# Operands of float32r products at multiples of 128 bytes; tables and masks of the second block made in the first block

## The chip, the cores and the metric

The kernel runs on one core of one Trainium2 chip. A time is the device time of one execution in microseconds (us); lower is better. Several executions are timed, and one is also recorded by the hardware profiler. TensorE (PE) multiplies matrices, with weight loads (PEld) beside it; VectorE (DVE), ScalarE (ACT) and GpSimd (POOL) do the element work; SyncE (SP) issues the DMAs. The on-chip buffer in which all operands of a product lie has 128 partitions; the offset of a tile is its start address within a partition.

## The reference

Two blocks are computed one after the other on 256 tokens of width 1024, two layers each. The first block has a context stream and a latent stream; its mixer joins attention, gated linear attention (GLA) and a convolution, and a gated feed-forward follows. The second block has a mixer of three kinds of attention and a feed-forward with a short convolution. It turns positions into rotary tables.

```python
def first_block(x, c, ctx, ...):
    ...
        x = _post(x, _latent_mixer(_modulate(x, sh1, sc1), mem, cos, sin, p), g1, ln1_g[l], ln1_b[l])
        x = _post(x, _ffn(_modulate(x, sh2, sc2), p), g2, ln2_g[l], ln2_b[l])
...
def second_block(x, positions, ...):
    cos, sin = rope_tables(positions)
    for l in range(DEPTH):
        h = rms_norm(x, attn_pre_norm[l])
        mix = hybrid_mixer(h, cos, sin, w_in[l], ...)
        x = x + rms_norm(mix, attn_post_norm[l])
        h = rms_norm(x, ffn_pre_norm[l])
        x = x + rms_norm(conv_ffn(h, w_up[l], ...), ffn_post_norm[l])
    return x
```

Here `_ffn` is `(silu(h @ w_gate) * (h @ w_up)) @ w_down` with a hidden width of 2816, and `rope_tables` is the cosine and sine of positions times eight frequencies.

## The kernel before

**Products in three parts.** A float32 product is made of three products in the type float32r. Each operand is split into a high part `hi` (rounded to float32r) and a low part `lo` (what is left), and `mm3` (L217) adds hi·hi (L220), hi·lo (L221) and lo·hi (L222) up in one PSUM tile. Weights come from DRAM in pieces of 128x1024 float32 (512 KB): `load` (L188) has SP start the DMA into one of four buffers `raw`; `weights` then has ScalarE cast it to `hi` (L210, three buffers) and VectorE subtract to `lo` (L213, two buffers, in halves of 512 columns). Activations are kept split too, as a pair of tiles in the buffer `b16`, which the profile calls `b`.

**Two shapes.** `gemm_f` takes 128 columns of weights as the stationary operand and streams 256 tokens of activations past it (out is channels by tokens; the profile's `g<-b,hi` with 128x256). `gemm_t` holds 128 tokens of activations and streams 512 columns of weights (`g<-hi,b` with 128x512). In names such as `g<-b,hi` out stands first, then the streamed operand, then the one that is held. Where activations of a feed-forward are in tiles `z`, `zz` or `h`, these stand in place of `b`; weights of the first block's feed-forwards also lie in free tiles `z`, `w` and `gp`.

**Pools and offsets.** Tiles lie in pools: `wts` (raw, hi, lo), `cst` and `sml` (constants and small tiles), `com` (b16 and rows), and one pool per stage: `first`, `mix0`/`mix1` (mixers), `ff`/`fx` (the feed-forwards of layers 0 and 1), `sec0` (second block). Within a pool tiles follow one another without gaps, so a tile of a width that isn't a multiple of 128 bytes moves those behind it. Where the built program puts the operands of the products, in bytes modulo 128 and modulo 256:

| operand | before, mod 128 | before, mod 256 | changed, mod 128 | changed, mod 256 |
|---|---|---|---|---|
| `hi`, `lo` in `wts` | 0 | 128 | 0 | 128 |
| `b` in `com` | 64 | 64 | 0 | 0 |
| `z` in `ff`, `w` and `zz` in `fx`, `hi` in `first` | 96 | 224 | 0 | 0 or 128 |
| tiles of the mixers in `mix` | 96 | 96 or 224 | 0 | 0 or 128 |
| `h` and others in `sec0` | 32 | 160 | 0 | 0 or 128 |
| `U` and others at the front of `first` | 64 | 192 | 0 | 0 or 128 |

**Order.** A scheduler with a timeline of its own decides the order of instructions on each engine when the program is built; code order and priorities guide it. Each engine then runs its row strictly in order, and SP issues DMAs in its row's order.

**The end of a mixer** (`post`, L1006 to L1051): for each of two token tiles and two halves of 512 columns, VectorE multiplies the product with the gate (L1019) and adds it to the residual (L1020); ScalarE squares it for the variance (L1024); GpSimd and VectorE make mean and inverse deviation of single columns (L1023 to L1034), and VectorE normalises (L1049, L1051). `ln` (L968, L976) normalises again for the next stage, and TensorE transposes (L991).

**Constants of the second block.** `positions` (L320) loads the positions, makes angles in eleven small VectorE operations and takes sine and cosine on ScalarE (L346, L347), which needs a table load. `consts2` (L349) casts the identity to bf16 (`identb`) and loads and casts two masks (`cmb`). Both are called at the start of the second block.

Of the kernel before, what the change touches and what calls it, by code (L numbers as in the profile page):

```python
# [9 lines left out]
F32 = mybir.dt.float32  # L10
F32R = mybir.dt.float32r
BF16 = mybir.dt.bfloat16
I32 = mybir.dt.int32
# [12 lines left out]
def together(**groups):  # L26
# [23 lines left out]
    'pt': dict(t=4),  # L50
}


# [112 lines left out]
class Core:  # L166
# [4 lines left out]
    def tile(self, pool, shape, dt=F32, tag=None, bufs=None):  # L171

        self.n += 1
        kind = pool.name.rstrip('0123456789')
        tag = SHARE.get(kind, {}).get(tag, tag)
        n = bufs or BUFS[kind].get(tag, 1)
        return pool.tile(list(shape), dt, name=f"{tag}_{self.n}", tag=tag, bufs=n)

# [138 lines left out]
class Second(Core):  # L317


    def positions(self, pos):  # L320
        nc = self.nc
        pi = self.tile(self.S, [128, 2], I32, 'pi')
        with nc.allow_non_contiguous_dma(reason="256 positions"):
# [4 lines left out]
        for t in range(2):  # L328
            nc.vector.tensor_scalar(ang[:, t], self.c('freq'), pf[:, t:t + 1], None, op0=ALU.mult)
        k = self.tile(self.S, [128, 2, 8], F32, 'angk')  # L330
# [18 lines left out]
    def consts2(self, cm):  # L349

        nc = self.nc
        self.identb = self.tile(self.P, [128, 128], BF16, 'identb')
        nc.vector.tensor_copy(self.identb, self.ident)
        self.cmb = []
        raw = self.load(cm)
        for t in range(2):
            b = self.tile(self.P, [128, 512], BF16, f'cmb{t}')
            nc.vector.tensor_copy(b, raw[:, t * 512:t * 512 + 512])
            self.cmb.append(b)
# [135 lines left out]
    def rope(self, pr, h0, n):  # L495
        nc = self.nc
        for t in range(2):
            x = pr[t][:, h0 * 64:(h0 + n) * 64].rearrange("p (h d) -> p h d", d=64)
            x1, x2 = x[:, :, 0:8], x[:, :, 8:16]
            cos = self.cs2[:, 0, t][:, None, :].to_broadcast([128, n, 8])  # L500
            sin = self.cs2[:, 1, t][:, None, :].to_broadcast([128, n, 8])
            a, b, c, d = [self.tile(self.P, [128, 14, 8], F32, 'rp')[:, :n] for _ in range(4)]
            nc.vector.tensor_mul(a, x1, cos)
            nc.vector.tensor_mul(b, x2, sin)
            nc.vector.tensor_mul(c, x2, cos)
            nc.vector.tensor_mul(d, x1, sin)
            nc.vector.tensor_sub(x1, a, b)
            nc.vector.tensor_add(x2, c, d)
# [203 lines left out]
    def attend(self, proj, pr, v, rb, src):  # L712
# [3 lines left out]

        ga = self.tile(self.P, [128, 2, 8, 3], F32, 'ga')
        lf, e, z = [self.tile(self.P, [128, 2, 4], F32, 'lf') for _ in range(3)]
        for t in range(2):
# [967 lines left out]
def build(tc, I, out):  # L1687
    nc = tc.nc
# [3 lines left out]
    with ExitStack() as es:  # L1692
# [16 lines left out]
        for l in range(2):  # L1709
            L = Layer1(l, I[f'w1{l}'], LAYOUT[0][l], I[f'row1{l}'])  # L1710
            L.a2 = I[f'a2{l}']
            L.vec = K.tile(K.C, [128, I[f'vec1{l}'].shape[1]], F32, 'vec1')
            nc.sync.dma_start(L.vec, I[f'vec1{l}'])
            L.cb2 = K.tile(K.C, [128, 8], F32, 'cb2')
            nc.vector.tensor_scalar(L.cb2, L.v('cb', 8), 2.0, None, op0=ALU.mult)
            Ls.append(L)
        with ExitStack() as e1:
# [18 lines left out]
            for l, L in enumerate(Ls):  # L1736
# [14 lines left out]
                with ExitStack() as e2:  # L1751
                    K.P = pool(e2, 'fx' if l else 'ff')
                    if l == 0:
# [3 lines left out]
                        for f in half:  # L1757
                            f()
                    else:
                        K.pend = left(K.ffn(L, X))  # L1760
        K.more = None
        with ExitStack() as e1:
# [7 lines left out]
            K.c = lambda n: c2[:, AT2[n][0]:AT2[n][0] + AT2[n][1]]  # L1770
            K.consts2(I['cm'])
            K.positions(I['pos'])
            for l in range(2):
# [17 lines left out]
```

## Time and profile before

| | us |
|---|---|
| median of 3 executions | 2732.79 |
| their range | 2726.75 to 2738.06 |
| profiled execution | 2729.63 |
| span of its instructions | 2727.8 |

The mean granted clock of TensorE in the profiled execution was 0.981 of full speed. In the profile the time of an engine is the sum of its instructions; TensorE's matmuls are pipelined, so the recorded duration of one is longer than the distance from its start to the next start. The chain that ended last is followed back from the last instruction, at each step to what released it. A number in brackets behind an instruction of the timeline is the idle time of its engine before it, with what ended it.

### The profile page before, as it was taken

How to read it: one execution, taken by the hardware profiler on the slowest of the kernel's cores; microseconds unless marked ns; L12 is line 12 of the kernel's file. 1: busy time of each engine (PE TensorE's matmuls, PEld its weight loads, DVE VectorE, ACT ScalarE, POOL GpSimd, SP SyncE). 2: the span in 40 equal slices, each digit the busy share in tenths (PEclk: the TensorE clock that was granted, in tenths of full speed). 3: DMA queues.
4: the chain of work that ended last, by engine and by line, in shares of the span. 5: the costliest groups of instructions: out<-in, count | busy, mean ns of one | idle time of the engine just before them, and what ended most of it. 6: DMA issues, size and time to landing. Idle time of an engine off the chain costs nothing.

```text
span 2727.8 us, 45641 instructions
## 1 busy us (share of the span) xinstructions
PE 2621.6 (96%) x17408; PEld 2271.2 (83%) x17408; DVE 1954.7 (72%) x3942; ACT 1383.3 (51%) x2524; POOL 137.8 (5%) x280
## 2 busy tenths in 40 slices
PE   7999999999999999999999999989989999999999
PEld 5977999977989888887797898979976699776997
DVE  4988977899967633355688997666676689556895
ACT  3555555545555422234754654544454566544663
POOL 0010011000001100001100100010010000000000
PEclk8999999999999999999999999989999999999999
DMA  7566456565535422222455433545554355542454
GB/s 255 187 224 206 163 178 211 185 208 180 179 116 206 173 93 93 93 93 100 154 167 201 160 120 117 172 152 186 186 183 148 110 170 196 172 160 93 163 193 155
DMA packets 127915, 443.34 MB, mean 163 GB/s; under 512 B 14888, under 2 KB 19112, under 8 KB 127696
## 3 DMA queue, kind: packets, MB, share of 16 engines
q1 hardware_dynamic: 127696, 440.43, 47.8%
q8 instruction: 137, 2.24, 0.3%
q14 instruction: 82, 0.67, 0.1%
HBM read 435.09 MB, written 5.28 MB: 161 GB/s over the span
## 4 chain that ended last, share of the span: by engine, by line
PE 88%; DVE 3%; DMA 3%; ACT 3%; issue 1%; POOL 1%; SPq 0%; DVEq 0%; POOLq 0%; ACTq 0%
PE g L221 21%; PE g L220 21%; PE g L222 20%; PE t L220 3%; PE t L222 3%; PE t L221 3%; DMA raw<-in_w_dram 3%; PE g L925 2%; PE t L1175 1%; PE t L1149 1%; PE t L1277 1%; PE t L1262 1%; PE t L1112 1%; PE t L1184 1%; PE g L663 1%
## 5 line engine op out<-in xcount | busy, mean ns | idle before, releaser
L213 DVE TENSOR_TENSOR lo<-raw,hi 128x512 fp32r<-128x512 f32 (+2 forms) x1280 | 824.8, 684 | 358.0 <-issue 157.3
L210 ACT CAST hi<-raw 128x1024 fp32r<-128x1024 f32 (+2 forms) x644 | 672.4, 1046 | 731.3 <-PE g L221 256.6
L220 PE MATMUL g<-b,hi 128*128 128x256 f32 (+1 forms) x2912 | 833.5, 288 | 4.4 <-ACT hi L210 3.9
L221 PE MATMUL g<-b,hi 128*128 128x256 f32 (+1 forms) x2912 | 829.4, 286 | 2.6 <-DVE b L311 2.5
L222 PE MATMUL g<-b,lo 128*128 128x256 f32 (+1 forms) x2912 | 823.4, 288 | 1.1 <-DVE lo L213 1.1
L220 PEld LDWEIGHTS g<-b,hi 128*128 128x128 f32 x2912 | 548.9, 189 | 15.1 <-ACT hi L210 4.3
L221 PEld LDWEIGHTS g<-b,hi 128*128 128x128 f32 x2912 | 549.4, 189 | 12.0 <-DVE b L311 3.9
L222 PEld LDWEIGHTS g<-b,lo 128*128 128x128 f32 x2912 | 542.1, 188 | 10.3 <-DVE lo L213 1.9
L1289 DVE SCALAR_TENSOR_TENSOR yc<-yc,vec,yc 128x256 f32<-128x256 f32 x720 | 345.4, 480 | 10.8
L221 PE MATMUL g<-lo,b 128*128 128x512 f32 (+2 forms) x712 | 271.4, 382 | 2.0 <-DVE lo L213 2.0
L222 PE MATMUL g<-hi,b 128*128 128x512 f32 (+2 forms) x712 | 264.7, 372 | 0.5 <-DVE b L314 0.4
L220 PE MATMUL g<-hi,b 128*128 128x512 f32 (+2 forms) x712 | 254.1, 377 | 11.2 <-ACT hi L210 5.7
L220 PEld LDWEIGHTS g<-hi,b 128*128 128x128 f32 x712 | 133.8, 191 | 38.5 <-ACT hi L210 6.5
L221 PEld LDWEIGHTS g<-lo,b 128*128 128x128 f32 x712 | 135.7, 191 | 30.7 <-DVE lo L213 6.2
L222 PEld LDWEIGHTS g<-hi,b 128*128 128x128 f32 x712 | 135.5, 190 | 22.2 <-DVE b L314 1.1
L220 PE MATMUL t<-b,hi 128*128 128x256 f32 (+1 forms) x336 | 112.6, 335 | 0.0
L221 PE MATMUL t<-b,hi 128*128 128x256 f32 (+1 forms) x336 | 112.6, 335 | 0.0
L222 PE MATMUL t<-b,lo 128*128 128x256 f32 (+1 forms) x336 | 112.4, 335 | 0.0
L477 DVE SCALAR_TENSOR_TENSOR s<-g,vec,s 128x255 f32<-128x255 f32 (+1 forms) x176 | 84.0, 478 | 6.0 <-ACT s L475 3.9
L925 PE MATMUL g<-raw,cs 128*32 128x256 f32 x768 | 67.7, 432 | 19.0 <-DMA raw<-in_w_dram 18.8
L221 PEld LDWEIGHTS t<-b,hi 128*128 128x128 f32 x336 | 63.7, 190 | 7.3
L220 PEld LDWEIGHTS t<-b,hi 128*128 128x128 f32 x336 | 63.2, 188 | 7.4
(421 smaller groups left out, 3928.7 us busy)
## 6 DMA issues: line engine op xcount, KB each, us to landing
raw<-in_w_dram SPq DMA_DIRECT2D x772, 512.0 KB, 3.8
b<-in_row_dram SPq DMA_DIRECT2D x16, 512.0 KB
b<-in_ctx_dram SPq DMA_DIRECT2D x4, 512.0 KB
ends<-st SPq DMA_DIRECT2D x8, 256.0 KB
st<-ends SPq DMA_DIRECT2D x8, 256.0 KB
b<-in_x_dram SPq DMA_DIRECT2D x4, 512.0 KB, 5.5
b<-ctx SPq DMA_DIRECT2D x4, 512.0 KB
raw<-in_w_dram SPq DMA_DIRECT2D x4, 426.0 KB
```

What stands on the lines that cost most here:

```text
L210: self.nc.scalar.copy(hi[:, :m], p)
L213: self.nc.vector.tensor_sub(lo[:, q], p[:, q], hi[:, q].bitcast(F32))
L220: t.matmul(ps, a[0], b[0], start=first, stop=False)
L221: t.matmul(ps, a[0], b[1], start=False, stop=False)
L222: t.matmul(ps, a[1], b[0], start=False, stop=last)
L477: nc.vector.scalar_tensor_tensor(c[:, m, j:], ps[:, m, :256 - j], cw[:, ft, 2 - j:3 - j], c[:, m, j:], op0=ALU.mult, op1=ALU.add)
L663: nc.tensor.matmul(ps[:, b], qk['nq', a * per + b][s, t * 128:t * 128 + 128], qk[kn, 0][s, :nk], start=False, stop=b == per - 1)
L925: m = nc.tensor.matmul(ps[32 * q:32 * q + 32, n * 256:n * 256 + 256], self.cs[:, h * 4 + q], raw[:, q * 256:q * 256 + 256], start=h == 0, ...
L1112: nc.tensor.matmul(p[:, h], kw[:, d, h * 128:h * 128 + 128], vg[:, h * 256:h * 256 + 256], start=True, stop=True)
L1149: nc.tensor.matmul(o, w, self.U[d][:, b * 256:b * 256 + n], start=d + i == 0, stop=d + i == 2)
L1175: nc.tensor.matmul(ps[:, a, h], G[h][b][:, a] if b < 3 else kT[:, h, ts], G[h][b][:, 2 + a], start=True, stop=True)
L1289: e.scalar_tensor_tensor(o, y[:, j:j + 256], w[:, j:j + 1], o, op0=ALU.mult, op1=ALU.add)
```

## The change

Tiles with two dimensions in the pools `first`, `mix`, `ff`, `fx` and `sec` are made wider, up to the next multiple of 128 bytes, and used in their first columns; three tiles that had more dimensions are written as padded two-dimensional ones, and `cb2` in `cst` gets 16 columns in place of 8. A scratch area at the front of the buffer is made 4096 bytes per partition in place of 16384. `consts2` and `positions` are called ahead of the feed-forward of the first block's second layer, and their tiles go to the pool `cst`; the frequencies get a DMA of their own.

```diff
--- before.py
+++ after.py
@@ -49,6 +49,11 @@
     'pg': dict(g=4),
     'pt': dict(t=4),
 }
+
+
+
+ALIGN = 128
+ALIGNED = ('first', 'mix', 'ff', 'fx', 'sec')
 
 
 class Layout:
@@ -174,7 +179,12 @@
         kind = pool.name.rstrip('0123456789')
         tag = SHARE.get(kind, {}).get(tag, tag)
         n = bufs or BUFS[kind].get(tag, 1)
-        return pool.tile(list(shape), dt, name=f"{tag}_{self.n}", tag=tag, bufs=n)
+        make = lambda s: pool.tile(s, dt, name=f"{tag}_{self.n}", tag=tag, bufs=n)
+        size = {F32: 4, F32R: 4, I32: 4, BF16: 2, U8: 1}[dt]
+        if kind in ALIGNED and len(shape) == 2 and shape[1] * size % ALIGN:
+            step = ALIGN // size
+            return make([shape[0], -(-shape[1] // step) * step])[:, :shape[1]]
+        return make(list(shape))
 
     @contextmanager
     def later(self, n):
@@ -317,8 +327,10 @@
 class Second(Core):
 
 
-    def positions(self, pos):
-        nc = self.nc
+    def positions(self, pos, freq):
+        nc = self.nc
+        fq = self.tile(self.S, [128, 32], F32, 'freq')[:, :8]
+        nc.sync.dma_start(fq, freq)
         pi = self.tile(self.S, [128, 2], I32, 'pi')
         with nc.allow_non_contiguous_dma(reason="256 positions"):
             nc.sync.dma_start(pi, pos.rearrange("o (t p) -> p (o t)", p=128))
@@ -326,7 +338,7 @@
         nc.vector.tensor_copy(pf, pi)
         ang = self.tile(self.S, [128, 2, 8], F32, 'ang')
         for t in range(2):
-            nc.vector.tensor_scalar(ang[:, t], self.c('freq'), pf[:, t:t + 1], None, op0=ALU.mult)
+            nc.vector.tensor_scalar(ang[:, t], fq, pf[:, t:t + 1], None, op0=ALU.mult)
         k = self.tile(self.S, [128, 2, 8], F32, 'angk')
         big = 1.5 * 2.0 ** 23
         nc.vector.tensor_scalar(k, ang, 1.0 / (2 * math.pi), big, op0=ALU.mult, op1=ALU.add)
@@ -349,12 +361,12 @@
     def consts2(self, cm):
 
         nc = self.nc
-        self.identb = self.tile(self.P, [128, 128], BF16, 'identb')
+        self.identb = self.tile(self.C, [128, 128], BF16, 'identb')
         nc.vector.tensor_copy(self.identb, self.ident)
         self.cmb = []
         raw = self.load(cm)
         for t in range(2):
-            b = self.tile(self.P, [128, 512], BF16, f'cmb{t}')
+            b = self.tile(self.C, [128, 512], BF16, f'cmb{t}')
             nc.vector.tensor_copy(b, raw[:, t * 512:t * 512 + 512])
             self.cmb.append(b)
 
@@ -499,7 +511,7 @@
             x1, x2 = x[:, :, 0:8], x[:, :, 8:16]
             cos = self.cs2[:, 0, t][:, None, :].to_broadcast([128, n, 8])
             sin = self.cs2[:, 1, t][:, None, :].to_broadcast([128, n, 8])
-            a, b, c, d = [self.tile(self.P, [128, 14, 8], F32, 'rp')[:, :n] for _ in range(4)]
+            a, b, c, d = [self.tile(self.P, [128, 112], F32, 'rp').rearrange("p (h n) -> p h n", n=8)[:, :n] for _ in range(4)]
             nc.vector.tensor_mul(a, x1, cos)
             nc.vector.tensor_mul(b, x2, sin)
             nc.vector.tensor_mul(c, x2, cos)
@@ -714,8 +726,8 @@
         nc = self.nc
         proj(5)
 
-        ga = self.tile(self.P, [128, 2, 8, 3], F32, 'ga')
-        lf, e, z = [self.tile(self.P, [128, 2, 4], F32, 'lf') for _ in range(3)]
+        ga = self.tile(self.P, [128, 48], F32, 'ga').rearrange("p (t h n) -> p t h n", h=8, n=3)
+        lf, e, z = [self.tile(self.P, [128, 8], F32, 'lf').rearrange("p (t h) -> p t h", h=4) for _ in range(3)]
         for t in range(2):
             nc.vector.tensor_add(z[:, t], pr[t][:, P2['ff']:P2['ff'] + 4], rb[:, 0:4])
             nc.vector.tensor_add(ga[:, t].rearrange("p h j -> p (h j)"), pr[t][:, P2['ng']:P2['ng'] + 24], rb[:, 4:28])
@@ -1711,7 +1723,7 @@
             L.a2 = I[f'a2{l}']
             L.vec = K.tile(K.C, [128, I[f'vec1{l}'].shape[1]], F32, 'vec1')
             nc.sync.dma_start(L.vec, I[f'vec1{l}'])
-            L.cb2 = K.tile(K.C, [128, 8], F32, 'cb2')
+            L.cb2 = K.tile(K.C, [128, 16], F32, 'cb2')[:, :8]
             nc.vector.tensor_scalar(L.cb2, L.v('cb', 8), 2.0, None, op0=ALU.mult)
             Ls.append(L)
         with ExitStack() as e1:
@@ -1757,6 +1769,9 @@
                         for f in half:
                             f()
                     else:
+                        K.consts2(I['cm'])
+                        n, m = AT2['freq']
+                        K.positions(I['pos'], I['cst2'][:, n:n + m])
                         K.pend = left(K.ffn(L, X))
         K.more = None
         with ExitStack() as e1:
@@ -1768,8 +1783,6 @@
             c2 = K.tile(K.P, list(CST2.shape), F32, 'cst2')
             nc.sync.dma_start(c2, I['cst2'])
             K.c = lambda n: c2[:, AT2[n][0]:AT2[n][0] + AT2[n][1]]
-            K.consts2(I['cm'])
-            K.positions(I['pos'])
             for l in range(2):
                 K.layer(X, K.vec2[l], I[f'w2{l}'], LAYOUT[1][l], I[f'row2{l}'], rows(out) if l else None)
             for t in range(2):
@@ -1780,7 +1793,7 @@
     import concourse.bacc as bacc
     from concourse.bass_utils import run_bass_kernel_spmd
 
-    nc = bacc.Bacc("TRN2", target_bir_lowering=False, num_devices=1)
+    nc = bacc.Bacc("TRN2", target_bir_lowering=False, num_devices=1, dynamic_dma_scratch_size=4096)
     ins = {f"in_{k}_dram": v for k, v in arrays({k: np.asarray(v) for k, v in inputs.items()}).items()}
     I = {k[3:-5]: nc.dram_tensor(k, v.shape, mybir.dt.from_np(v.dtype), kind="ExternalInput").ap() for k, v in ins.items()}
     out = nc.dram_tensor("out_0_dram", (256, D), F32, kind="ExternalOutput").ap()
```

The built program has as many instructions on TensorE, VectorE, ScalarE and GpSimd as before; SP has one DMA more. TensorE's row is the same but for a few neighbouring products of GLA in the first block's second mixer. Lines of the changed kernel stand 10 to 13 lines lower in the file (L1019 of before is L1031).

VectorE at the end of the mixer that precedes the last feed-forward of the first block (some 1795 to 1801 us of the profile), before:

```order
L1019 TENSOR_TENSOR th_18823<-g_18745,b_3106_18741 128x512
L213 TENSOR_TENSOR lo_18851<-raw_18848,hi_18850 128x512 x2
L1019 TENSOR_TENSOR th_18831<-g_18746,b_3106_18741 128x512
L1020 SCALAR_TENSOR_TENSOR b_1720_10318,pmv_18743<-b_1720_10318,th_18823 128x512
L213 TENSOR_TENSOR lo_19025<-raw_19022,hi_19024 128x512 x2
L1020 SCALAR_TENSOR_TENSOR b_1721_10319,pmv_18744<-b_1721_10319,th_18831 128x512
L1019 TENSOR_TENSOR th_18928<-g_18839,b_3106_18741 128x512
L213 TENSOR_TENSOR lo_19032<-raw_19029,hi_19031 128x512 x2
L1020 SCALAR_TENSOR_TENSOR b_1720_10318,pmv_18743<-b_1720_10318,th_18928 128x512
```

and in the changed kernel:

```order
L1031 TENSOR_TENSOR th_18823<-g_18745,b_3106_18741 128x512
L223 TENSOR_TENSOR lo_18851<-raw_18848,hi_18850 128x512 x2
L1031 TENSOR_TENSOR th_18831<-g_18746,b_3106_18741 128x512
L1032 SCALAR_TENSOR_TENSOR b_1720_10318,pmv_18743<-b_1720_10318,th_18823 128x512
L370 CAST cmb_3145_18931<-raw_18929 128x512
L370 CAST cmb_3146_18933<-raw_18929 128x512
L1032 SCALAR_TENSOR_TENSOR b_1721_10319,pmv_18744<-b_1721_10319,th_18831 128x512
L223 TENSOR_TENSOR lo_19056<-raw_19053,hi_19055 128x512 x2
L1031 TENSOR_TENSOR th_18959<-g_18839,b_3106_18741 128x512
L223 TENSOR_TENSOR lo_19063<-raw_19060,hi_19062 128x512 x2
L1032 SCALAR_TENSOR_TENSOR b_1720_10318,pmv_18743<-b_1720_10318,th_18959 128x512
```

The two casts of masks now stand between the residual sums of the two token tiles, and the second sum comes behind them.

ScalarE at the same place, before (`th` is the square of a half, `hi` a cast of weights):

```order
L210 CAST hi_19024<-raw_19022 128x1024
L210 CAST hi_19031<-raw_19029 128x1024
L1024 ACTIVATE th_18823,pmv_18743<-b_1720_10318,pmv_18743 128x512
L210 CAST hi_19087<-raw_19085 128x1024
L1024 ACTIVATE th_18831,pmv_18744<-b_1721_10319,pmv_18744 128x512
L210 CAST hi_19094<-raw_19092 128x1024
L1024 ACTIVATE th_18928,pmv_18743<-b_1720_10318,pmv_18743 128x512
L1024 ACTIVATE th_18957,pmv_18744<-b_1721_10319,pmv_18744 128x512
```

and in the changed kernel:

```order
L220 CAST hi_19055<-raw_19053 128x1024
L1036 ACTIVATE th_18823,pmv_18743<-b_1720_10318,pmv_18743 128x512
L220 CAST hi_19062<-raw_19060 128x1024
L1036 ACTIVATE th_18831,pmv_18744<-b_1721_10319,pmv_18744 128x512
L220 CAST hi_19118<-raw_19116 128x1024
L220 CAST hi_19125<-raw_19123 128x1024
L1036 ACTIVATE th_18959,pmv_18743<-b_1720_10318,pmv_18743 128x512
L1036 ACTIVATE th_18988,pmv_18744<-b_1721_10319,pmv_18744 128x512
```

The first square has moved up by one cast, and the third and fourth squares have two casts of weights right ahead of them where one stood ahead of the third. On SP the mask's load stands ahead of the load of `raw_19053`, the first of these casts.

ScalarE at the start of the program (some 18 to 27 us), before:

```order
L929 COPY am_129<-g_104 128x512
L976 ACTIVATE b_31_171<-b_31_171,s_n_34_179,s_n_38_186 128x512 x2
L929 COPY am_163<-g_138 128x512
L996 ACTIVATE th_206<-t_205,mod_103,mod_137 128x256
L996 ACTIVATE th_216<-t_215,mod_103,mod_137 128x256
L310 CAST b_33_178<-th_206 128x512
```

and in the changed kernel:

```order
L941 COPY am_129<-g_104 128x512
L988 ACTIVATE b_31_171<-b_31_171,s_n_34_179,s_n_38_186 128x512 x2
L941 COPY am_163<-g_138 128x512
L359 ACT_TABLE_LOAD
L359 ACTIVATE cs_3152_18952<-ang_18941 128x16
L358 ACTIVATE cs_3152_18952<-angn_18953 128x16
L1008 ACTIVATE th_206<-t_205,mod_103,mod_137 128x256
L1008 ACTIVATE th_216<-t_215,mod_103,mod_137 128x256
L320 CAST b_33_178<-th_206 128x512
```

The table load with the cosine and the sine of the angles has come in ahead of the first modulation. At the second block's start they are gone from between the moves of transposed tiles, and nothing takes their place there.

## Rows read from the trace of the kernel before

**Rows 1.** The page's first part: engine, busy us, share of the span, x instructions.

```profile
PE 2621.6 (96%) x17408; PEld 2271.2 (83%) x17408; DVE 1954.7 (72%) x3942; ACT 1383.3 (51%) x2524; POOL 137.8 (5%) x280
```

**Rows 2.** The page's chain that ended last: share of the span by engine.

```profile
PE 88%; DVE 3%; DMA 3%; ACT 3%; issue 1%; POOL 1%; SPq 0%; DVEq 0%; POOLq 0%; ACTq 0%
```

**Rows 3.** Groups by form, TensorE, whole span: line, op, out<-in, xcount | busy us, mean ns.

```profile
L220 PE MATMUL g<-b,hi 128*128 128x256 f32 x2736 | 767.9, 283 | 4.4 <-ACT hi L210 3.9 <-ACT b L310 0.5
...
L222 PE MATMUL g<-hi,b 128*128 128x512 f32 x552 | 218.2, 396 | 0.0
...
L220 PE MATMUL t<-b,hi 128*128 128x512 f32 x160 | 63.0, 394 | 0.0
...
L222 PE MATMUL g<-hi,h 128*128 128x512 f32 x152 | 60.1, 396 | 0.0
...
L221 PE MATMUL t<-lo,z 128*128 128x512 f32 x88 | 34.7, 396 | 0.0
```

**Rows 4.** Windows: us; busy us (x records) of PE, PEld, DVE, ACT, POOL; granted clock; DMA.

```profile
50.00:350.00 300.00, 292.71 (x2193) 256.06 (x2192) 266.16 (x583) 165.94 (x374) 14.65 (x22) 0.99 0.57 192
886.00:899.00 13.00, 13.00 (x58) 10.66 (x58) 9.89 (x16) 7.79 (x11) 0.00 (x0) 1.00 0.57 195
921.10:925.60 4.50, 4.50 (x40) 4.50 (x39) 3.42 (x7) 0.56 (x1) 1.82 (x3) 1.00 0.59 229
1000.00:1150.00 150.00, 150.00 (x645) 120.21 (x644) 52.20 (x80) 35.02 (x40) 0.00 (x0) 1.00 0.27 92
1163.00:1284.00 121.00, 121.00 (x519) 97.41 (x518) 62.86 (x91) 46.93 (x54) 9.77 (x18) 1.00 0.27 93
1850.00:1940.00 90.00, 90.00 (x763) 90.00 (x763) 53.60 (x84) 39.63 (x44) 0.00 (x0) 1.00 0.55 185
2200.00:2300.00 100.00, 100.00 (x885) 100.00 (x884) 94.44 (x175) 64.95 (x91) 0.00 (x0) 1.00 0.57 192
```

**Rows 5.** Timeline, TensorE, 1274.6 to 1277.6 us: start us, duration us, line, op, out<-in.

```profile
1274.71 0.39 PE L220 MATMUL g<-z,z 128*128 128x512 f32 x1
...
1275.40 0.39 PE L220 MATMUL g<-z,z 128*128 128x512 f32 x1
...
1277.22 0.39 PE L222 MATMUL g<-z,z 128*128 128x512 f32 x1
1277.44 0.40 PE L221 MATMUL g<-lo,z 128*128 128x512 f32 x1
```

**Rows 6.** Groups by form, TensorE, 2003 to 2005.7 us.

```profile
L221 PE MATMUL g<-w,zz 128*128 128x512 f32 x4 | 1.6, 389 | 0.0
```

**Rows 7.** Groups by form, VectorE, whole span.

```profile
L213 DVE TENSOR_TENSOR lo<-raw,hi 128x512 fp32r<-128x512 f32 x1268 | 819.8, 686 | 357.0 <-issue 157.1 <-PE g L222 65.4 <-PE t L222 41.8
```

**Rows 8.** Timeline, all engines, 2012.3 to 2015 us.

```profile
2012.56 0.75 DVE L358 CAST cmb<-raw 128x512 bf16<-128x512 f32 x2
...
2014.85 0.48 PE L385 MATMUL t<-cst,b 128*128 128x128 f32 x1 [5.68 <-ACT b L376]
```

**Rows 9.** Timeline, all engines, 2019.6 to 2025.7 us.

```profile
2019.68 1.28 ACT L347 ACT_TABLE_LOAD   x1
...
2020.87 0.18 DVE L345 TENSOR_SCALAR angn<-angn 128x16 f32<-128x16 f32 x1
...
2020.98 0.22 ACT L347 ACTIVATE cs<-ang 128x16 f32<-128x16 f32 x1
...
2025.62 0.40 PE L221 MATMUL g<-lo,b 128*128 128x284 f32 x1 [0.33 <-DVE lo L213]
```

**Rows 10.** Timeline, all engines, 23 to 27 us.

```profile
25.38 0.17 DVE L936 SCALAR_TENSOR_TENSOR mod<-g,vec 128x8 f32<-128x8 f32 x1 [3.50 <-PE g L933]
25.58 1.02 ACT L996 ACTIVATE th<-t,mod,mod 128x256 f32<-128x256 f32 x2 [1.35 <-DVE mod L936]
```

**Rows 11.** Timeline, ScalarE, 1792 to 1804 us.

```profile
1795.47 1.05 ACT L210 CAST hi<-raw 128x1024 fp32r<-128x1024 f32 x1 [3.87 <-DMA raw<-in_w_dram]
1797.61 1.05 ACT L210 CAST hi<-raw 128x1024 fp32r<-128x1024 f32 x1 [1.08 <-DMA raw<-in_w_dram]
```

**Rows 12.** Timeline, TensorE, 1802 to 1814 us.

```profile
1812.63 1.39 PE L991 MATMUL t<-cst,w 128*128 128x128 f32 x4 [10.05 <-ACT w L976]
```

## Prediction

> **What bounds the kernel now.** I read the page first: TensorE is busy 96% of the span, VectorE 72%, ScalarE 51% [rows 1], and 88% of the chain that ended last is TensorE [rows 2]. So the end moves with the time of one matmul, or with the few places where TensorE waits. Next, the groups by form: nearly all of it is the three products of `mm3` in two shapes, 256 and 512 columns streamed [rows 3]. Then I looked for the time from one start to the next, since the recorded length (276 to 398 ns) overlaps with its neighbours. A stretch in which TensorE is always busy gives it: (length of the stretch + length of one record) / records, as a record that only reaches into the stretch is counted too. That view shows that equal products don't cost the same [rows 4]:
>
> - 512 columns, activations `b` streamed over `hi`/`lo`: (150 + 0.39)/645 = 233.2 ns. `hi`/`lo` over `z`: (121 + 0.4)/519 = 233.9, and `hi` over `h` has the records of these, 395 to 397 ns [rows 3]. `hi`/`lo` over `b`: (13 + 0.39)/58 = 230.9, and over longer runs of starts 229.1.
> - 256 columns, `b` over `hi`/`lo`: (90 + 0.28)/763 = 118.3 in the first block's last feed-forward, (100 + 0.28)/885 = 113.3 in the second block's. One form, one pair of buffers, two speeds, each held for a whole stage. `b` over `z`, where weights lie in `z`: (4.5 + 0.28)/40 = 119.5.
>
> Two groups of rows tell what the 512-column cost hangs on. In `z` against `z` the first three starts, after a streamed `lo`, are still (1275.40 − 1274.71)/3 = 230 ns apart; from 1275.40 on, (1277.22 − 1275.40)/8 = 227, until a `lo` is streamed again [rows 5]. `w` against `zz` has the same short records, 389 ns [rows 6]. In both pairs streamed and stationary operand lie at the same offset in 128 bytes (both at 96); the slower pairs above differ by 64 (`com`/`wts`), 96 (`wts`/`ff`) or 32 (`wts`/`sec`). Names, columns and neighbours don't separate them, this offset does. So 226.7 and 113.3 ns are the floors shown here.
>
> **Alignment, the main term.** The change puts all these operands at 0 modulo 128, so every product gets the relation that only `z`/`z`, `w`/`zz` and a few products of the second block have now. Excess over the floor, by counts from [rows 3] (the three lines of a form have equal counts):
> - `b` over `hi`/`lo`, 512 columns: 3 x (160 + 144; one of the two rows stands) = 912, x (233.2 − 226.7) = 5.9 us.
> - `hi`/`lo` over `b`, 512: 3 x 552 = 1656, x (229.1 − 226.7) = 4.0 us.
> - over `z` (88 and 72, three times, 480) x 7 = 3.4 us; over `h` 3 x 152 = 456, x 6.5 = 3.0 us; some 400 of smaller groups (`zz` among them) x 6.5 = 2.6 us.
> - 256 columns: 3 x 2736 = 8208. Following the starts matmul by matmul where the granted clock is full and nothing waits, 7,100 of them average 115.2 ns, between the two stages' 113.3 and 118.3: 1.9 ns, 13.5 us. About 1,500 other 256-column products (`t<-b,hi` in the same stages, `U`, operands in `first`) run 3 to 5 ns over: 5 us.
>
> Sum 37 us, half of it 512 columns. Not all reaches the end: VectorE makes the `lo` parts, 1268 times 686 ns [rows 7], and its durations don't depend on these offsets in the trace. It is busy 266 of the 300 us from 50 to 350, 89%, and 94% in the second block's feed-forward [rows 4]. The latter is at the floor already; in the others it has 11% left against the 2% that TensorE would gain, but the room comes in pieces, and each piece that isn't there turns a gain into a wait for `lo`. TensorE's other work isn't touched. I take three quarters: **−28 us**; bounds −37 (all of it, TensorE being the chain) and −17 (only the 512-column part, almost all of it in stretches where VectorE is 35 to 76% busy [rows 4]). The padding itself adds no instruction.
>
> Beside this stands a rule: the Trainium skill, "TensorE: Matmul & The Clock Gate", Step-by-step, has two independent read ports of the buffer, so that loading the next weights takes nothing from the matmul that runs. By it the placing of one operand against the other would be worth nothing and the sum 0; the rows above, 227 against 233 ns for the same shape, speak against it, though not to the last doubt, as they were not made by moving one operand alone.
>
> **Constants, where they leave.** The two mask casts (0.75 us) and `identb` (0.22) ran from 2012.42, while the path was with ScalarE and GpSimd: TensorE starts at 2014.85, after 5.68 us for ScalarE's normalised tile [rows 8]. Their cover is that chain; removal is worth 0. The sine's table load (1.28) and two activations (0.22 each) sat among the moves of transposed tiles, with the moves and the `hi` cast behind them up to 1.7 us late for it; TensorE's gap that follows is 0.33 us [rows 9]. Gain 0 to 1.7, I take 0.5, nearer to the gap.
>
> **Constants, where they arrive.** (a) At the start: the eleven small VectorE operations, 0.18 us each where they run now [rows 9] and so 2.0 together, come into VectorE's idle of 3.50 us before 25.38. `freq` adds one small DMA to SP's row ahead of a weight load; four loads are in flight there, so I cost it at nothing, and at one such operation's 0.4 us if that cover is gone. ScalarE's table load and two sines, 1.28 + 0.44, stand in an idle of 1.35 before 25.58 [rows 10]: up to +0.4 us for the next activation. A later activation then needs its own table back, 1.28 at most. Together 0 to +2.1, I take +0.6. (b) Before the last feed-forward: the mask load takes the place of a weight load in SP's row, and every weight load behind it comes one ring slot later. ScalarE already waits 3.87 and 1.08 us for such loads there, with 2.1 us from one to the next (1795.47, 1797.61) [rows 11]. The two mask casts queue on VectorE ahead of the second tile's residual sum; they wait for the mask load, and the `lo` parts and residual sums behind them wait too, 0.75 us, of which idle of VectorE takes some. One more `hi` cast now stands ahead of the last squares, at 1.05 us. TensorE has done its last product by then regardless and waits 10.05 us for this very chain [rows 12], so a delay that survives counts whole: 0 to +2.1 us, I take +0.9.
>
> Together constants cost +1.0 us, with bounds −1.7 and +4.2. Sum: 2729.63 − 28 + 1 = 2702.6 for an execution like the profiled one. The profiled execution lies 3.2 us below the median of the three, 2732.79; the same distance gives 2705.8, so **2706 us**.
>
> **Rivals.**
> - *Only 512 columns gain.* The 256-column stages have two speeds at one relation, so their speed may be set by something else (by how the stream last started) and stay as it is on the whole. For it: 113.3 and 118.3 with the same buffers. Against: with a relation that holds no conflict there is nothing to lock into. 18 us of 512 columns, of which nine tenths arrive: −16 + 1, **2718**. The same figure comes if VectorE keeps all of the 256-column gain.
> - *Nothing changes,* because the offset is not the cause: the `z` and `w` operands are not only aligned with each other, their weights also lie in their tiles long before they are used, unlike those in `hi` and `lo`. Then only constants move: **2734**. By the Trainium skill (the page above) this is the expected outcome. The same figure results where 512-column products gain 18 us and the 256-column ones all lock at the slow 118: (118.3 − 115.2) x 8208 = +25 us, less the cover in VectorE's stages.
> - *A new conflict: slower.* `com` lies at 0 and `wts` at 128 modulo 256 after the change; the pairs at the floor agree modulo 256 too (224 and 224), and no product of before has a difference of exactly 128. If two operands half a period apart collide as those 32 apart do, the place is the 8208 products of 256 columns: at the 119.5 ns of `b` over `z` [rows 4] they cost 4.3 x 8208 = +35 us, while 512 columns stay where they are, and constants add 1: **2769**. If 512 columns gain their 16 us all the same, it is slower than before from 1.8 ns more per 256-column product onwards ((16 − 1)/8208), and by over 0.5% from 3.5 ns. Against it: a pattern of 64-byte or 128-byte lines would make 128 as good as 0.
> - *The change doesn't do what it says:* excluded, since the build of the changed kernel shows every such operand at 0 modulo 128.
>
> **How the numbers follow.** About 0.5% of this time, 13.7 us, is what a measurement can tell from no change, so faster is under 2719. Forecast 2690 to 2712: 0.46. Only 512 columns (2712 to 2725): 0.22, three quarters of it under 2719. Nothing or cancelled (2725 to 2742): 0.20. Slower: 0.12. Faster 0.46 + 0.16 = 0.62, same 0.26, slower 0.12. The range leaves the slower case out and the best 5% below: 2691 to 2739.
>
> **What would show it.** Right: `z` rows and `b`-over-`hi` rows of 512 columns with records near 389 to 390 ns instead of 394 to 397; 645 records of the window at 1000 us become about 663 in 150 us; the stage that had 763 records in 90 us has 795; the second block's feed-forward unchanged at 276. VectorE's share rises, and `lo` appears more often as the releaser of TensorE. TensorE's wait before the last feed-forward is 10 to 12 us. Wrong: records of 281 or more in the second block's feed-forward (new conflict), or 394 where both operands are aligned (offset not the cause); a wait of over 13 us at the last feed-forward would make the move of constants dearer than I took it.

## The result, and the profile after

The changed kernel takes 2770.83 us (median of 5 executions, 2764.94 to 2776.63) against 2732.79 before: ratio 1.0139, 95% interval 1.0117 to 1.016. It is slower, by 38 us. The profiled execution of the changed kernel has a span of 2769.0 us, against 2727.8.

The page's busy line and its chain that ended last, changed kernel, answer to [rows 1, 2]:

```profile
PE 2665.7 (96%) x17408; PEld 2312.8 (84%) x17408; DVE 1958.7 (71%) x3942; ACT 1386.2 (50%) x2524; POOL 138.7 (5%) x280
...
PE 89%; DMA 3%; ACT 3%; DVE 2%; issue 1%; POOL 1%; SPq 0%; DVEq 0%; POOLq 0%; ACTq 0%
```

TensorE is busy 44 us longer, and as large a share of the chain. So the time went into the products themselves, not into a wait. The windows that answer to [rows 4] (us; busy us and records of PE, PEld, DVE, ACT, POOL; granted clock; DMA): `b` over `hi`/`lo` with 512 columns, `hi`/`lo` over `z`, the first block's last feed-forward, and the second block's feed-forward.

```profile
1020.00:1160.00 140.00, 140.00 (x604) 113.53 (x603) 49.60 (x76) 32.92 (x37) 0.00 (x0) 1.00 0.28 94
1185.00:1300.00 115.00, 115.00 (x497) 93.34 (x496) 60.50 (x88) 46.47 (x54) 10.23 (x18) 1.00 0.28 93
1870.00:1960.00 90.00, 90.00 (x757) 90.00 (x756) 53.87 (x84) 39.76 (x44) 0.00 (x0) 1.00 0.56 184
2230.00:2330.00 100.00, 100.00 (x836) 100.00 (x835) 89.25 (x165) 62.19 (x87) 0.00 (x0) 1.00 0.56 185
```

With the prediction's own division, (length + one record)/records, these are 232.4, 232.2, 119.3 and 120.0 ns; before they were 233.2, 233.9, 118.3 and 113.3. These 512-column products gained 1 to 2 ns in place of 6.5, and the 256-column ones of the second block lost 6.7. The groups by form in the second block's feed-forward (2200 to 2300 us before, 2230 to 2330 us after) show it in the record too, 282 to 285 ns where it was 276:

```profile
L220 PE MATMUL g<-b,hi 128*128 128x256 f32 x295 | 80.5, 276 | 0.0
```

```profile
L230 PE MATMUL g<-b,hi 128*128 128x256 f32 x278 | 77.9, 283 | 0.0
L232 PE MATMUL g<-b,lo 128*128 128x256 f32 x280 | 76.2, 282 | 0.0
```

Over the whole trace, from one start to the next at full clock with nothing waited for, the 256-column products of `com` over `wts` average 119.2 ns (7124 of them) against 115.2 (7061). Summed over all of that form, halved clock included, that is 30 us of the 41 that the span grew. Weights streamed over `com` (512) add 3, which the other 512-column products give back. Most of the rest comes within 500 products of the second block's first mixer, where the changed kernel falls another 8.8 us behind. The granted clock there, before (2026 to 2200 us) and after (2040 to 2220 us):

```profile
2026.00:2200.00 174.00, 162.97 (x949) 124.24 (x948) 111.31 (x284) 90.29 (x207) 3.29 (x8) 0.97 0.41 137
```

```profile
2040.00:2220.00 180.00, 169.18 (x898) 125.49 (x897) 108.28 (x283) 87.67 (x210) 3.31 (x8) 0.90 0.37 123
2134.00:2156.00 22.00, 22.00 (x78) 12.33 (x77) 8.62 (x24) 6.62 (x16) 0.00 (x0) 0.50 0.33 125
```

It is 0.97 before and 0.90 after: one stretch of 24 us at the lower level (1.2 GHz; the last line lies inside it), where before there was one of 3.4. In both traces it begins behind 1.7 us of idle TensorE among small products; why it lasted longer in one is not shown. The profiled executions of two kernels below have a stretch of 24 us as well, those of 2768.97 and 2731.08 us, a slow and a fast one, so it does not decide which kernel is slow. It takes its part of the 41 us all the same. Matched one by one between the two traces, the 256-column products of `com` over `wts` grew by 31.5 us at full clock, all other products of these two shapes by under 1 in sum, and products at which one trace had the lower clock by 10. The mean granted clock of the changed kernel's five executions is 0.974 to 0.976, and in 18 of 23 later ones of the kernel before it is 0.977 to 0.981. So up to some 10 of the 38 us may be the clock's, and about 30 are the products'.

The moved constants show little. ScalarE at the mixer's end, which answers to [rows 11], waits 4.88 us for its weights in place of 3.87, as each load stands one place later in SP's row, behind that of the masks:

```profile
1816.63 1.05 ACT L220 CAST hi<-raw 128x1024 fp32r<-128x1024 f32 x1 [4.88 <-DMA raw<-in_w_dram]
...
1818.30 1.03 ACT L220 CAST hi<-raw 128x1024 fp32r<-128x1024 f32 x1
...
1820.40 1.98 ACT L220 CAST hi<-raw 128x1024 fp32r<-128x1024 f32 x2
```

TensorE's wait behind that place, [rows 12] before with 10.05 us, is 10.25:

```profile
1832.50 1.40 PE L1003 MATMUL t<-cst,w 128*128 128x128 f32 x4 [10.25 <-ACT w L988]
```

### The profile page after: what moved, and what is told of

Same layout as the page of the kernel before. It is cut to its first block, busy times and chain, and to the rows that moved or that the text cites. A ratio compares the mean times of both kernels' runs of the same rounds, so it can differ in the third digit from the quotient of the medians.

```text
span 2769.0 us, 45643 instructions
## 1 busy us (share of the span) xinstructions
PE 2665.7 (96%) x17408; PEld 2312.8 (84%) x17408; DVE 1958.7 (71%) x3942; ACT 1386.2 (50%) x2524; POOL 138.7 (5%) x280
## 4 chain that ended last, share of the span: by engine, by line
PE 89%; DMA 3%; ACT 3%; DVE 2%; issue 1%; POOL 1%; SPq 0%; DVEq 0%; POOLq 0%; ACTq 0%
PE g L231 21%; PE g L230 21%; PE g L232 21%; DMA raw<-in_w_dram 3%; PE t L230 3%; PE t L231 3%; PE t L232 3%; PE g L937 1%; PE t L1187 1%; PE t L1161 1%; PE t L1289 1%; PE t L1274 1%; PE t L1124 1%; PE g L675 1%; PE t L1196 1%
## 5 line engine op out<-in xcount | busy, mean ns | idle before, releaser
L230 PE MATMUL g<-b,hi 128*128 128x256 f32 (+1 forms) x2912 | 843.7, 292 | 2.6 <-ACT hi L220 2.1
L231 PE MATMUL g<-b,hi 128*128 128x256 f32 (+1 forms) x2912 | 840.8, 290 | 2.3 <-DVE b L321 2.2
L232 PE MATMUL g<-b,lo 128*128 128x256 f32 (+1 forms) x2912 | 833.7, 291 | 1.1 <-DVE lo L223 1.1
L232 PEld LDWEIGHTS g<-b,lo 128*128 128x128 f32 x2912 | 543.7, 189 | 10.1 <-DVE lo L223 1.9
L231 PE MATMUL t<-b,hi 128*128 128x256 f32 (+1 forms) x336 | 113.0, 336 | 0.0
L230 PE MATMUL t<-b,hi 128*128 128x256 f32 (+1 forms) x336 | 113.0, 336 | 0.0
L232 PEld LDWEIGHTS t<-b,lo 128*128 128x128 f32 x336 | 63.4, 189 | 7.1
L231 PEld LDWEIGHTS t<-b,hi 128*128 128x128 f32 x336 | 63.5, 189 | 7.0
```

The source lines that it names most:

```text
L230: t.matmul(ps, a[0], b[0], start=first, stop=False)
L231: t.matmul(ps, a[0], b[1], start=False, stop=False)
L232: t.matmul(ps, a[1], b[0], start=False, stop=last)
```

## The experiments

Two parts were changed at once, so the first question was which of them cost the time; the second, what about the offsets costs it; the third, whether slabs of products alone (long rows of equal products, with nothing beside them) explain the kernel. Three theories are named before their own experiment comes: by A a difference of 128 bytes between streamed and held operand is bad and 0 is good; by B every multiple of 128 is bad for 256 columns and good for 512; by C the offset is not the cause.

**Constants alone.** `ALIGNED = ()`, the padded tiles back to their old widths, and filler so that every operand starts where it did modulo 256:

```diff
-ALIGNED = ('first', 'mix', 'ff', 'fx', 'sec')
+ALIGNED = ()
...
-        fq = self.tile(self.S, [128, 32], F32, 'freq')[:, :8]
+        fq = self.tile(self.S, [128, 64], F32, 'freq')[:, :8]
```

> Only the constants are moved; every tile of the products starts at the same offset modulo 256 as before. Theories A and B: the alignment is the whole loss, this runs at 2731 to 2738 us (ratio 0.999 to 1.002), 256-column products 113 to 118 as before. Rival (constants cost most of it, through the later weight loads): 2755 or more.

Measured: 2731.53 us, ratio 0.9987 (0.9971 to 1.0003). The second block's feed-forward has its 885 records in 100 us as before [rows 4], and the wait behind the mixer is 10.3 us:

```profile
2200.00:2300.00 100.00, 100.00 (x885) 100.00 (x884) 94.75 (x175) 65.75 (x92) 0.00 (x0) 1.00 0.56 195
```

```profile
PE t L1003 <- ACT w L988: 10.3, 1, 10.3
```

Moving the constants is worth nothing that can be measured, −8 to +1 us.

**Alignment alone, activations 128 bytes from the weights.** `consts2` and `positions` back at the second block's start, with 128 bytes of padding so that all offsets are those of the changed kernel:

```diff
+        K.pad = K.tile(K.C, [128, 32], F32, 'pad')
...
+            K.consts2(I['cm'])
+            K.positions(I['pos'])
```

> Only the alignment; constants are made at the second block's start as before; activations start 128 bytes from the weights modulo 256, as in the changed kernel. Theories A and B: 2765 to 2772 us, ratio 1.012 to 1.015, 256-column products at 119 to 120 ns. Rival (constants): 2735.

Measured: 2768.97 us, ratio 1.0121 (1.009 to 1.0153). The alignment is the whole loss.

**Alignment alone, activations and weights at the same offset.** The same kernel without the padding; all starts are still multiples of 128, but `com` and the stages' pools move by 128 bytes, so that the difference modulo 256 is 0 (for a few tiles of the mixers 128).

> Only the alignment, without the 128 bytes of padding of the other kernel: activations and weights both start at 128 modulo 256 (difference 0), all other tiles moved with the activations. Theory A: 256-column products at 113.3 and 512-column ones at 227, 2695 to 2715 us. Theory B: 256 columns stay at 119 to 120, 512 columns at 227, 2745 to 2765 us.

Measured: 2750.04 us, ratio 1.007 (1.0052 to 1.0087): 19 us faster than with 128, and still slower than before. Its windows, `b` over `hi`/`lo` with 512 columns, `hi`/`lo` over `z`, and the second block's feed-forward:

```profile
1008.00:1158.00 150.00, 150.00 (x664) 124.24 (x663) 54.48 (x84) 36.58 (x42) 0.00 (x0) 1.00 0.28 97
1180.00:1290.00 110.00, 110.00 (x487) 91.13 (x486) 59.39 (x86) 45.13 (x53) 10.01 (x18) 1.00 0.28 97
2215.00:2315.00 100.00, 100.00 (x835) 100.00 (x835) 88.98 (x166) 61.18 (x87) 0.00 (x0) 1.00 0.53 184
```

226.5, 226.7 and 120.1 ns. The 512-column products of these windows are at the floor; those of weights over `com` came down only from 230.0 to 228.8 on the mean, which the difference alone does not explain. The 256-column ones are at their worst. So 38 us of loss in the one shape ((119.8 − 115.2) x 8208) outweigh 17 of gain in the other, and TensorE waits some 5 us less. Theory A is gone: 0 is bad for 256 columns as well.

**The products alone.** A kernel that holds nothing but slabs of products in the kernel's own pattern: 96 of 256 columns (activations streamed), 48 of 512 with weights streamed, 48 of 512 with activations streamed, for 22 distances between the two tiles, twice each, and 10 more with both tiles moved.

```python
for m in range(8):
    for k in range(4):
        s = slice(m * 128, m * 128 + 128)
        todo += [(hi(k)[:, s], b(0, k)), (hi(k)[:, s], b(1, k)), (lo(k)[:, s], b(0, k))]
```

> This kernel leaves the whole computation out: it runs only slabs of 96 (or 48) float32r products as the big products of the kernel do them (three products each, fresh weights every time), with nothing else on the chip, and moves the activations against the weights by a given number of bytes. Weights start at 128 modulo 256 (0 in the sweep). Theory A (a difference of 128 bytes modulo 256 between streamed and held operand collides, 0 does not): 256-column products at 113.3 ns with differences 0 and 256, 119 to 120 at 128, 113 to 118 at 64. Theory B (every difference that is a multiple of 128 is bad for 256 columns and good for 512): 256 columns at 119 to 120 with 0, 128, 256, 512, and 512 columns at 227 there. Theory C (the offset is not the cause, other traffic is): every slab at one speed.

Measured, TensorE's windows inside slabs (us, busy us and records, clock, DMA share, GB/s). 256 columns at differences 0, 64, 112, 128, 192, then 192 again with both tiles moved by 32 bytes; then 512 columns with weights streamed at 0 (a stretch of several slabs in a row) and 128:

```profile
85.00:96.00 11.00, 11.00 (x94) 1.00 0.00 1
130.20:141.20 11.00, 11.00 (x96) 1.00 0.01 1
164.50:175.20 10.70, 10.70 (x97) 1.00 0.00 0
175.40:186.60 11.20, 11.20 (x97) 1.00 0.01 1
221.00:231.60 10.60, 10.60 (x96) 1.00 0.01 2
...
436.70:447.40 10.70, 10.70 (x97) 1.00 0.00 0
815.00:885.00 70.00, 70.00 (x310) 1.00 0.00 0
...
964.20:975.00 10.80, 10.80 (x48) 1.00 0.00 0
```

DMA and the other engines are silent, the clock is full, and the speeds are all there. In a window as short as one slab, a record more or less at the edge moves the quotient by 1% (256 columns) or 2% (512), so the table goes by the starts. From start to start, mean of a slab behind its first eight products (two values where its two passes differ by over 0.5 ns; difference is streamed minus held operand in bytes, modulo 256):

| difference | 256 columns, ns | 512, weights streamed | 512, activations streamed |
|---|---|---|---|
| 0 | 120.0 | 226.7 | 226.7 |
| 16 | 118.7, 116.7 | 226.7 | 231.7 |
| 32 | 116.7, 117.8 | 233.2 | 233.3 |
| 48 | 118.3 | 233.2, 232.0 | 233.3 |
| 64 | 117.8 | 229.0 | 228.9 |
| 80 | 120.0 | 230.0 | 231.1 |
| 96 | 120.0 | 233.2 | 233.4 |
| 112 | 113.4 | 233.3 | 231.1 |
| 128 | 118.7 | 233.4, 232.5 | 232.3 |
| 144 | 118.6, 113.3 | 233.2 | 233.3 |
| 160 | 117.3, 118.7 | 234.3 | 234.3 |
| 176 | 119.3 | 232.0 | 233.4 |
| 192 | 113.3 | 233.3 | 233.3 |
| 208 | 119.2 | 233.2 | 234.7 |
| 224 | 118.3 | 233.4 | 233.3 |
| 240 | 117.2 | 226.9, 233.4 | 226.7, 233.4 |

Distances of 256, 512, 1024, 2048 and 4096 bytes give the numbers of 0, and 320 those of 64. Moving both tiles by 32 or 64 changes nothing but for 32 bytes, where the passes differ anyhow. So it is the difference modulo 256 that counts, not where a tile lies, and the two shapes want different ones. Why the difference costs time, no run here shows. Neither theory had that: B was right that 0 and 128 are bad for 256 columns, and wrong that 128 is good for 512. C is gone.

The table reads back into both kernels. Before, `com` at 64 streamed over `wts` at 128 is 192: 113.3 for 256 columns, 233.3 for 512 (measured 233.3); `wts` over `com` is 64: 229.0 (about 230); over `ff` 160: 234.3 (234.3); over `sec` 224: 233.4 (233.3). After, `com` over `wts` is 128: 118.7 (119.2), and 232.3 (232.4). The kernel before lay, for its most frequent product, at one of the two best places of the table.

**Activations alone moved, in both directions.** In the kernel before, filler moves only `com`, from 64 to 0 modulo 256; in the changed kernel, only `com`, from 0 back to 64:

```diff
+        K.pad = K.tile(K.S, [128, 48], F32, 'pad')
...
+            K.pad2 = K.tile(K.A, [128, 16], F32, 'pad2')
```

> The kernel before with the activations alone moved, to 0 modulo 256 (128 bytes from the weights); all other tiles, and the constants, as before. Theory E: 256-column products at 118.7 to 120, 512-column ones of weights over activations at 232; 2758 to 2768 us. Rival (the loss comes from the other pools): 2735.

> The changed kernel with the activations alone put back by 64 bytes (192 bytes from the weights modulo 256, as before); every other tile keeps the start that the change gave it. Theory E (the speed follows from the difference modulo 256 as the slabs alone gave it): 256-column products back to 113.3 to 117.8, 512-column ones of weights over activations 229; 30 us come back, 2736 to 2744 us. Rival (the absolute offsets or the other pools' tiles matter): 2755 or more.

Measured: 2766.70 us, ratio 1.0136 (1.0108 to 1.0165), for the first; 2731.08 us, ratio 0.9993 (0.9977 to 1.0009), for the second (there the filler is 64 and 192 bytes). The second block's feed-forward of the first kernel, and that and the first block's last one of the second:

```profile
2225.00:2320.00 95.00, 95.00 (x803) 95.00 (x802) 85.65 (x159) 59.17 (x83) 0.00 (x0) 1.00 0.56 186
```

```profile
2200.00:2300.00 100.00, 100.00 (x885) 100.00 (x884) 94.67 (x176) 65.90 (x93) 0.00 (x0) 1.00 0.59 195
1850.00:1940.00 90.00, 90.00 (x794) 89.91 (x793) 55.81 (x87) 41.39 (x47) 0.00 (x0) 1.00 0.59 195
```

118.7 in the one, 113.3 and 113.7 in the other. 64 bytes between two buffers make the change's loss, and take it back; this answers the rival for which the other pools or the absolute offsets matter. The second came out 5 us below what was expected for it, and at least part of it is that 256-column products settled at the fast speed more often than before, at 114.7 ns on the mean in place of 115.2: in the first block's last feed-forward 794 records in 90 us, where the kernel before has 763 at the same difference [rows 4]. Which speed a stage takes at 192 was the next question.

**What decides between two speeds.** Slabs of 256 columns again, each entered behind a break: 1 to 4 small products, or a wait.

> Leaves the whole computation out: only slabs of 96 float32r products of 256 columns, at differences (streamed minus held operand, modulo 256) of 192, 112, 64 and 128 bytes, each entered behind a different break: one to four small products of 64, 128, 192, 284 or 512 columns, or a wait for VectorE and ScalarE. Theory D (at 192 bytes, the difference of before, a stream has two speeds that it can settle in, and what breaks the stream decides which): most slabs at 192 run at 113.3 ns, some at 117 to 118. Rival (the speeds seen before have another cause, such as the other engines' traffic): every slab at 192 at 113.3 whatever precedes it. Both: 128 at 118.6 and 64 at 117.8.

Measured: at 192 bytes 18 of the 34 slabs run at 113.3 ns and 16 at 117.8, and the seven that open the kernel with no break between them all keep 117.8. At 112 bytes all 34 end at 113.3. At 64, 28 of 34 run at 117.8 and 6 at 113.3, where 117.8 throughout was expected; at 128, all at 118.7 or 120.0. TensorE's windows of four slabs: 192 behind one product of 512 columns, 192 behind two of them, 112 behind one, 64 behind three:

```profile
175.50:186.00 10.50, 10.50 (x92) 1.00 0.00 0
187.50:197.40 9.90, 9.90 (x90) 1.00 0.01 2
368.50:378.60 10.10, 10.10 (x92) 1.00 0.00 0
586.50:596.50 10.00, 10.00 (x91) 1.00 0.01 2
```

(10.5 + 0.28)/92 = 117.2 and (9.9 + 0.28)/90 = 113.1: the same products, the same tiles. The third window holds the first microseconds behind the break as well, (10.1 + 0.28)/92 = 112.8, and is at the floor. The fourth is (10 + 0.28)/91 = 113.0. Theory D holds for 192, and 64 and 128 have two speeds too. What in a break decides is open: at 192, 11 of the 17 ways in led to the same speed in both passes, but behind one product of 64 columns the slab went fast in the first and slow in the second.

**A version with operands placed by the slabs.** Two steps. First `com` at 64 and `wts` at 128 as before, and all tiles of the stages' pools at 128, padded to 256:

```diff
-ALIGN = 128
+ALIGN = 256
...
+        K.pad = K.tile(K.S, [128, 16], F32, 'pad')
...
+            K.pad2 = K.tile(K.A, [128, 16], F32, 'pad2')
```

> A version that is chosen from the slabs: activations at 64 and weights at 128 modulo 256 as before (difference 192, 113.3 ns for 256 columns), and all tiles of the stages' pools at 128, as the weights (difference 0, 226.7 ns for 512 columns; 192 for the 256-column products that hold them). Constants moved as in the change. Theory E: 512-column products over z, zz and h at 227 instead of 233 to 234, 256-column ones over z and the first pool at 113 to 118 instead of 119 to 120: 8 to 12 us less than before, 2720 to 2726 us. Rival (512-column gains are taken back by waits for the weights): 2730.

Measured: 2721.09 us, ratio 0.9963 (0.9946 to 0.9979), as expected. `hi`/`lo` over `z` has (120 + 0.39)/529 = 227.6 ns, the last few `b` products ahead of them among the records; the second block is unchanged:

```profile
2190.00:2290.00 100.00, 100.00 (x884) 100.00 (x884) 94.49 (x175) 66.02 (x93) 0.00 (x0) 1.00 0.59 195
1155.00:1275.00 120.00, 120.00 (x529) 99.11 (x528) 62.24 (x84) 50.48 (x56) 8.16 (x16) 1.00 0.31 102
```

Then each tile of activations starts where its own products want it: 112 from the weights where 256 columns are streamed, 0 where it is held or streamed in 512:

```diff
+    def b16(self, skip):
+        return self.tile(self.A, [128, 4096 + 64], F32R, 'b16')[:, skip:skip + 4096]
+
+    def pair(self, skip=44):
...
-        hi, lo = self.pair()
+        hi, lo = self.pair(16 if apart else 44)
```

> The version before it with one thing more: each tile of activations starts where the slabs were fastest and had one speed only. Activations that are streamed in 256 columns lie 112 bytes behind the weights modulo 256 (113.3 ns after every break), those that are only held, or streamed in 512 columns, at the same offset as the weights (226.7 ns). What is left over the floor by the slabs: 800 products of weights over activations at 233, about 5 us, and 860 others of 256 columns, 5 us; 29 of the 39 us of before should be gone from TensorE's products. Theory E with the gain arriving in full: 2702 to 2705 us. With VectorE's lo parts keeping a quarter to a third of what the 256 columns give: 2706 to 2714. Rival (the two speeds at 192 are not cured by 112 inside the kernel): 2720 as the version before it.

Measured: 2711.14 us, ratio 0.9934 (0.9913 to 0.9954): by the ratio 18 us faster than before, and 60 faster than the change. Of what was expected, that is the case in which part of the gain stays behind (2706 to 2714). Windows of `b` over `hi`/`lo` with 512 columns, of `hi`/`lo` over `z`, of the first block's last feed-forward and of the second block's:

```profile
995.00:1140.00 145.00, 145.00 (x641) 120.11 (x640) 52.96 (x81) 35.90 (x41) 0.00 (x0) 1.00 0.29 97
1165.00:1275.00 110.00, 110.00 (x487) 91.10 (x486) 55.93 (x77) 44.92 (x50) 8.16 (x16) 1.00 0.30 102
1840.00:1930.00 90.00, 90.00 (x794) 89.91 (x793) 55.88 (x87) 41.39 (x46) 0.00 (x0) 1.00 0.59 194
2190.00:2290.00 100.00, 100.00 (x883) 99.92 (x882) 94.55 (x175) 64.84 (x92) 0.00 (x0) 1.00 0.59 195
```

226.8, 226.7, 113.7 and 113.6 ns, against 233.2, 233.9, 118.3 and 113.3 in [rows 4]. Over the whole trace the excess over the floor of products that follow one another at full clock fell from 38.0 us to 14.2, and the span by 20.1.

## Why the prediction was wrong

**What bounds the kernel** was right: TensorE's products, and their start-to-start time depends on where the two operands lie. The slabs show it with nothing else on the chip. The rule that was set beside it, two read ports that do not disturb each other (the Trainium skill, "TensorE: Matmul & The Clock Gate", Step-by-step), would have made the placing worth nothing. That is not borne out for these products: in the slabs a product of 256 columns takes 113.3 to 120.0 ns with nothing changed but the distance of its operands.

**The step that failed** is the one from [rows 4 to 6] to the main term: "The change puts all these operands at 0 modulo 128, so every product gets the relation that only `z`/`z`, `w`/`zz` and a few products of the second block have now." It went beyond the rows twice. The pairs at 227 ns agree modulo 256, and the change gives most products a difference of 128: 512 columns went to 232.4, not to 226.7. And the pairs all have 512 columns; nothing in the trace showed a float32r product of 256 columns at difference 0, where it is slowest (120.0). "226.7 and 113.3 ns are the floors" was true as numbers. But 113.3 was shown at a difference of 192, and by the prediction's own offsets that row spoke against one rule for both shapes.

**The main term** was forecast at −28 us, three quarters of 37, and came out at some +32 in the trace, whose span grew by 41 with the clock's part. 256 columns: −13.5 forecast at the start to start, +28 measured (119.2 against 115.2 on 7,100, and 30 on all). 512 columns: −18 forecast; about nothing for all of them, as `wts` over `com` lost some 2.5 ns each and the rest gained 0.4 to 2.

**The share that arrives** was set at three quarters, on account of VectorE. The changed kernel could not test it, as there was no gain. The last version lost 23.8 us of excess; its span is 20.1 us shorter, and by the ratio of its times 13 to 24 us arrive. In the trace TensorE's waits grew by 2 us, and products at the lower clock by 3. So three quarters is not shown wrong, and that VectorE takes the rest is not shown either.

**The two speeds** were seen, and one rival gave the right reason ("by how the stream last started"). The breaks show this. They also answer what was set against it, "with a relation that holds no conflict there is nothing to lock into": at 112 there is indeed one speed, but the change's 128 is no such relation, and there both of its speeds (118.7 and 120.0) are slow.

**The slower rival** was right in its place and nearly in its price: 119.5 ns on the 8208 products and 512 columns unchanged gave 2769; measured are 119.2 and 2770.83. That the times agree to 2 us is partly luck, as the products account for about 32 us and the lower clock for part of the rest. It had a chance of 0.12. What it lacked for more was a reason to doubt that multiples of 128 are all alike, and its own sentence held one, as no product of before had a difference of exactly 128. What it took from the pairs at 227, that 0 is good, is wrong for 256 columns.

**Constants**: forecast +1.0 with bounds −1.7 and +4.2; measured alone −8 to +1, which is too wide to tell +1.0 from nothing. The one step that has a row of its own, the wait at the mixer's end, grew by 0.2 to 0.3 us in place of 0.9.

**The range**, 2691 to 2739, left the slower case out, and that is the case that came.

## What to carry to other kernels

A rate that is read from a few pairs of operands holds for that shape and that distance; before a layout is changed for thousands of products, run the products alone over the distances, which took one kernel of 2.4 ms. Pad to a relation between two buffers that a measurement chose, not to round addresses: here 64 bytes of distance were worth 35 us in one kernel and 40 in the other. And where one form shows two speeds at one layout, look for a layout with only one before counting on the faster.

## What the runs showed of the hardware

- The time of a float32r product with fresh weights each time depends on the difference of the streamed and the held operand's start, modulo 256 bytes: 113.3 to 120.0 ns for 256 columns, 226.7 to 234.7 for 512. Steps of 16 bytes were tried. Neither the absolute start (moved by 32 and 64 bytes) nor distances of 256 to 4096 bytes matter. In a kernel with other work, weights streamed over activations at difference 0 took 228.8 on the mean, not 226.7 (the kernel of 2750.04 us).
- The two shapes have different best differences: 0 for 512 columns (226.7), where 256 columns are slowest (120.0); 112 and 192 for 256 columns (113.3), where 512 take 231 to 233.
- At 192 bytes a stream of 256-column products settles at 113.3 or at 117.8 ns and keeps it until something breaks it: 18 and 16 of 34 slabs. At 64 bytes it has the same two speeds (6 and 28 of 34), at 128 bytes 118.7 or 120.0. At 112 bytes all 34 settled at 113.3.
